# Gathering the tokens of eight experts at a time, with another order of steps around it

## The chip, the cores and the metric

One NeuronCore of a Trainium2 chip runs the kernel as one program. The metric is the device time of one launch in microseconds (us). A profiled execution of the kernel before gives, for each engine, what it did when: TensorE (PE, with its weight loads as PEld), VectorE (DVE), ScalarE (ACT), GpSimd (POOL) and SyncE (SP), which issues the transfers of weights.

## The reference

A trunk of two layers over 256 tokens of width 1024, all in f32. Each layer has a token mixer and a channel mixer, and both are modulated by six vectors that a product of a conditioning vector with `ada_w` gives:

```python
mod = silu(c) @ ada_w[l] + ada_b[l]              # sh1, sc1, g1, sh2, sc2, g2
h = rmsnorm(x, norm_mix_g[l]) * (1 + sc1) + sh1
proj = h @ w_in[l]                               # split among three kinds of attention heads
mix = concat([differential, sliding_window, dilated]) @ w_out[l]
x = x + g1 * mix
h = rmsnorm(x, norm_ffn_g[l]) * (1 + sc2) + sh2
x = x + g2 * moe(h)                              # after both layers: rmsnorm(x, final_norm_g)
```

`moe` has 4 groups of 4 experts. A router takes the best group of a token and in it the best two experts; each expert is `(silu(h @ w_gate) * (h @ w_up)) @ w_down` with w_gate and w_up 1024 x 512 and w_down 512 x 1024. Each of the 16 experts has some tokens, so all weights are read once: 283.63 MB of transfers in all.

## The kernel before

**Weights.** `Body.units` (L345) writes down, in the order of use, every piece of weights ("unit", mostly 512 KB). `Ring` (L137) issues them in that order on SP's queue. A unit goes to one of 29 ring tiles ("big"); the next transfer starts when the oldest unit is finished and its slot is free. Since SP issues in order, a unit that waits for its place holds up all behind it. Some units of the expert part don't take ring slots: HALVES (L32) names units, counted from the layer's first gate unit, that go to two tiles of the pool "w" (17 tiles of 128x512), and LENT (L33) units that go to a work tile of the pool "k" (11 tiles of 128x1024). Ring slots, "w" and "k" tiles serve everything else too.

**Order.** TensorE's instructions run in the order in which the code writes them. ScalarE's, VectorE's, GpSimd's and SP's are put in order by a planner with a cost model; `issue_after(i)` forces what is in its block behind instruction i of the same engine. For the mixer the written order is a list of names: START (before layer 1's mixer: S = split a unit of w_in into a high and a low fp32r part on ScalarE and VectorE, L761; X = transposes of x, L663; a = one step of an `ada_w` product for later modulation, four matmuls of 512 columns on two units, L450; R = the factor of the norm, L672), MIX (P = a unit of the input projection, twelve fp32r products; A, B, C = the three attentions) and TAIL (CT = transposes of q and k of the dilated heads, CF their scores and softmax, AM = transposes of the differential heads' output, B V/O and C V/O = probabilities times values, W = a unit of the output projection, d = a step of `ada_w` for the channel mixer, L524). The same list fixes the place of every unit in the stream (`pieces`, L416).

START of layer 1 is a generator (L729): it is advanced during the last expert of layer 0, whose last two quarters of columns (`combined`, L1451) are added to x between its steps.

**Router** (L1171). x is transposed and multiplied with the router's weights into one PSUM bank; four partial results are summed by a second product (`pl`) from an SBUF copy (L1195). `e` is a step of `ada_w` as `d` is. While the norm's factor r is made, ScalarE makes the high fp32r part of x * r (`xhi`, L1206); VectorE ranks the logits, counts each token's place in its expert (`pos`, at most 64 an expert), and makes the low part (`xlo`, L1246).

**Experts** (L1309). They run in 8 pairs j. `gather` turns tokens into slots by products with a one-hot matrix (VectorE's comparison of `pos` with 1..64, L1303): for each four experts, before pair j = 0, 2, 4, 6, 32 products of 256 columns, evicted with the modulation into two k tiles. Then come for each pair gate (`first`, L1361), the transposes and the down products of the pair before (L1407), `places` (transposes of the one-hots, L1338), up (L1361) and `combine`, which sends the results back to tokens by the transposed one-hots (L1428).

Of the kernel before, what the change touches and what calls it, by code (L numbers as in the profile page):

```python
# [9 lines left out]
F32 = mybir.dt.float32  # L10
F32R = mybir.dt.float32r
BF16 = mybir.dt.bfloat16
I32 = mybir.dt.int32
AF = mybir.ActivationFunctionType
OP = mybir.AluOpType
# [4 lines left out]
S = 256  # L20
KT = 8
NE = 16
CAP = 64
# [6 lines left out]
SCRATCH = 512  # L30
AHEAD = 2
HALVES = ((21, 27), (21, 27))  # L32
LENT = (((27, 32), (61, 62), (64, 65), (67, 68)),) * 2  # L33
NW = 17
A_START = 24

# [10 lines left out]
C_Z, C_CAUSAL, C_ID, C_CFAR, C_IOTA, C_LOW = (_AT[n].start for n in ("Z", "CAUSAL", "ID", "CFAR", "IOTA", "LOW"))  # L47
# [6 lines left out]

START = ["X c c R c c S00".split(), "S00 S01 X0 X1 S02 X2 X3 a a R".split()]
TAIL = """
CT0 CT1 d d d d CF0 AM1 CF1
W0 BV0 BV1 W1 BV2 BV3 BO0 BV4 W2 BV5 CV0 W3 BO1 CV1 CV2 W4 CO0 W5 W6  # L60
"""
MIX = [("""
P00 c P01 c P10 c c N P11 P02 P03 a a P12 L AT0 P13 a a AT1
# [2 lines left out]
P40 P41 BF1 a P42 AM0 P43 BF2 a a a H2 a  # L66
""" + TAIL).split(), ("""
P00 P01 P02 P03 P10 P11 AT0 P12 AT1 P13 AF0
P20 a AF1 P21 a AF2 P22 a P23 a
P30 AV0 P31 AV1 a AO0 BT0 P32 AV2 BT1 AO1 P33 AO2 BF0 a  # L70
P40 P41 BF1 P42 G2 AM0 P43 BF2 H2
""" + TAIL).split()]
# [127 lines left out]
class Body:  # L200
# [694 lines left out]
    def mixer(self, l):  # L895
        nc, ring, mod = self.nc, self.ring, self.mod
# [218 lines left out]

        acc = {}

        def wout(k, t):
            if k == 0 and t == 0:
                for tt in range(2):  # L1120
                    for hf in range(2):
                        acc[tt, hf] = self.acc.tile([128, 512], F32, name="acc")
            self.split_upto(l, 20 + k + AHEAD)
            mix, i = (T["mixa"], k) if k < 2 else (T["mixb"], k - 2) if k < 6 else (T["mixc"], k - 6)
            for hf in range(2):
                self.product(acc[t, hf], [m[:, i, blk(t)] for m in mix],
                             [p[:, 512 * hf:512 * hf + 512] for p in self.parts[20 + k]], k == 0, k == KT - 1)

        def w(k):
            if k < 6:  # L1130
                for t in range(2):
                    wout(k, t)
                return
            self.new_squares()
            for t in range(2):
                for k in (6, 7):
                    wout(k, t)
                for hf in range(2):
                    c = slice(512 * hf, 512 * hf + 512)
                    d = self.w()  # L1140
                    nc.vector.tensor_tensor(out=d, in0=acc[t, hf], in1=mod[l, 2][:, c], op=OP.mult)
                    nc.vector.tensor_tensor(out=self.x[t][:, c], in0=self.x[t][:, c], in1=d, op=OP.add)
                    self.square(t, hf, 512 * hf, 512 * hf + 512)
# [4 lines left out]
        for what in MIX[l]:  # L1148
            name, n = what.rstrip("0123456789"), what.lstrip("ABCFGHLMNOPSTVWacd")
# [21 lines left out]
    def router(self, l, dense):  # L1171
        nc, small = self.nc, self.one
        xt = {}
        for t in range(2):
            for i in range(2):
                xt[t, i] = self.w().rearrange("p (j c) -> p j c", j=4)
                p = self.transposes([self.x[t][:, 512 * i + 128 * j:512 * i + 128 * j + 128] for j in range(4)],
                                    _Named(self.acc, "acc"))
# [6 lines left out]
        ps = self.ps.tile([128, 512], F32, name="s")  # L1185
        for t in range(2):
            for i in range(2):
                for j in range(4):
                    nc.tensor.matmul(ps[32 * j:32 * j + 32, 128 * t:128 * t + 128], lhsT=self.wrs[:, 4 * i + j],
                                     rhs=xt[t, i][:, j], start=(i == 0), stop=(i == 1))  # L1190
        self.common(l, "e")
        pl = [ps[:, 256 + 20 * t:276 + 20 * t] for t in range(2)]
        for t in range(2):
            lt = self.w()[:, 0:128]
            nc.scalar.copy(lt, ps[:, 128 * t:128 * t + 128])  # L1195
            nc.tensor.matmul(pl[t], lhsT=lt, rhs=self.cb[:, C_SEL:C_SEL + 20], start=True, stop=True)
        self.common(l, "e")
        r = self.rstds(self.squares())
        if not dense:

            self.xhi, self.xlo = [[self.wk.tile([128, KT, 128], F32R, name="k") for t in range(2)] for _ in range(2)]
            xk = [self.x[t].rearrange("p (k c) -> p k c", k=KT) for t in range(2)]
            for i in range(2):
                for t in range(2):
                    c = slice(4 * i, 4 * i + 4)
                    nc.scalar.activation(self.xhi[t][:, c], xk[t][:, c], AF.Copy, scale=r[t])  # L1206
        lg = small.tile([128, 2, 20], F32, name="lg")
        for t in range(2):
            nc.vector.scalar_tensor_tensor(out=lg[:, t], in0=pl[t], scalar=r[t],
                                           in1=self.rbias, op0=OP.mult, op1=OP.add)  # L1210
# [7 lines left out]
                                in1=lf.unsqueeze(3).to_broadcast([128, 10, 4, 4]), op=OP.is_ge)  # L1218
# [8 lines left out]
        if not dense:  # L1227
            ab = small.tile([128, 2, 4, 4], BF16, name="ab")
            nc.vector.scalar_tensor_tensor(out=ab, in0=rank[:, :, 1:5], scalar=1.5, op0=OP.is_lt, op1=OP.mult,
                                           in1=og.unsqueeze(3).to_broadcast([128, 2, 4, 4]))  # L1230
# [8 lines left out]
                                           in1=ab, op0=OP.add, op1=OP.mult)  # L1239
# [57 lines left out]

    def one_hot(self, b):

        one = self.w(F32R).rearrange("p (t e s) -> p t e s", t=2, e=4)  # L1300
        iota = self.cb[:, C_IOTA:C_IOTA + CAP].unsqueeze(1).to_broadcast([128, 4, CAP])
        for t in range(2):
            i = self.nc.vector.tensor_tensor(out=one[:, t], in0=iota, op=OP.is_equal,  # L1303
                                             in1=self.pos[:, t, 4 * b:4 * b + 4].unsqueeze(2).to_broadcast([128, 4, CAP]))
        self.hot[b] = one.rearrange("p t e s -> p t (e s)")
        return i


    def moe(self, l):  # L1309
        nc, ring = self.nc, self.ring  # L1310
# [1 line left out]
        sh, sc, g = self.mod[l, 3], self.mod[l, 4], None  # L1312
        xt, G, U, pts, gates, act = {}, {}, {}, {}, {}, {}

        def gather(b, k2):

            if k2 == 0:
                if b:
                    self.one_hot(b)
                xt[b] = [self.wk.tile([128, 4, S], F32, name="k") for _ in range(2)]  # L1320
            one = hot[b]
            p = self.pt.tile([128, 512], F32, name="t").rearrange("p (k s) -> p k s", k=2)
            for kk in range(2):
                n = 0
                for t in range(2):
                    for part in (self.xhi, self.xlo):
                        nc.tensor.matmul(p[:, kk], lhsT=part[t][:, 2 * k2 + kk], rhs=one[:, t],  # L1327
                                         start=(n == 0), stop=(n == 3))
                        n += 1
            for kk in range(2):  # L1330
                self.modulate(xt[b][k2 // 2][:, 2 * (k2 % 2) + kk], p[:, kk], sc, sh, 2 * k2 + kk, 1 - k2 % 2)

        def places(j):

            p = self.pt.tile([128, 512], F32, name="t")
            hf = hot[j // 2][:, :, 128 * (j % 2):128 * (j % 2) + 128]
            for t in range(2):
                nc.tensor.transpose(p[:, 128 * t:128 * t + 128], hf[:, t].bitcast(F32), self.ident)  # L1338
            for t in range(2):
                nc.tensor.matmul(p[:, 256:288], lhsT=hf[:, t],  # L1340
                                 rhs=self.ghl[:, t].rearrange("p u e -> p (u e)"), start=(t == 0), stop=(t == 1))
            pt = self.w(F32R)[:, 0:S]
            nc.scalar.copy(pt, p[:, 0:256])
            gs = self.small.tile([128, 1], F32, name="gs")
            for u in range(2):
                e = 2 * j + u
                r = slice(64 * u, 64 * u + 64)
                nc.vector.tensor_reduce(out=gs[r], in_=p[r, 256 + e:288:16], axis=AX.X, op=OP.add)
            pts[j], gates[j] = pt, gs

        def first(kind, store, j, hh):

            if hh == 0:
                store[j] = self.ps.tile([128, 512], F32, name="s")
            x = xt[j // 2]
            w = [ring.take2((kind, l, 2 * j + u, hh)) for u in range(2)]
            for kk in range(2):
                k = 2 * hh + kk
                for u in range(2):
                    c = (j % 2) * 128 + 64 * u  # L1360
                    nc.tensor.matmul(store[j][64 * u:64 * u + 64, :], lhsT=x[k // 4][:, k % 4, c:c + 64],  # L1361
                                     rhs=w[u][kk], start=(k == 0), stop=(k == KT - 1))
            ring.done(2)

        def gates_of(j, between=None):

            if j % 2:
                first("gate", G, j, 0)
                first("gate", G, j, 1)
                if between:  # L1370
                    between()
            else:
                gather(j // 2, 0)
                gather(j // 2, 1)
                first("gate", G, j, 0)
                gather(j // 2, 2)
                if between:
                    between()
                first("gate", G, j, 1)
                gather(j // 2, 3)  # L1380
            first("gate", G, j, 2)
            first("gate", G, j, 3)
            silu(j)
# [267 lines left out]
```

## Time and profile before

| | us |
|---|---|
| median of 3 runs | 758.12 (757.98 to 759.51) |
| profiled execution | 756.71 |
| its span, first to last instruction | 754.8 |
| TensorE busy | 712.9 |
| VectorE busy | 342.6 |
| ScalarE busy | 211.7 |
| GpSimd busy | 65.7 |
| TensorE's weight loads busy (beside the products) | 372.4 |

A busy time counts an engine's instructions and not what they waited for. Matmul records overlap, so TensorE's busy time is no measure of how near it is to its peak. Of the transfers, the weight queue (q1) carried 282.33 MB; the mean rate over the span was 376 GB/s. TensorE's clock has two levels in this profile, granted 1.00 (2.4 GHz) and 0.50 (1.2 GHz).

### The profile page before, as it was taken

How to read it: one execution, taken by the hardware profiler on the slowest of the kernel's cores; microseconds unless marked ns; L12 is line 12 of the kernel's file. 1: busy time of each engine (PE TensorE's matmuls, PEld its weight loads, DVE VectorE, ACT ScalarE, POOL GpSimd, SP SyncE). 2: the span in 40 equal slices, each digit the busy share in tenths (PEclk: the TensorE clock that was granted, in tenths of full speed). 3: DMA queues.
4: the chain of work that ended last, by engine and by line, in shares of the span. 5: the costliest groups of instructions: out<-in, count | busy, mean ns of one | idle time of the engine just before them, and what ended most of it. 6: DMA issues, size and time to landing. Idle time of an engine off the chain costs nothing.

```text
span 754.8 us, 10672 instructions
## 1 busy us (share of the span) xinstructions
PE 712.9 (94%) x3790; PEld 372.4 (49%) x3790; DVE 342.6 (45%) x940; ACT 211.7 (28%) x482; POOL 65.7 (9%) x89
## 2 busy tenths in 40 slices
PE   6899898999999999999989999897999999999993
PEld 2565675754353353353346668675435335344341
DVE  4587697354042333133357869637213313332234
ACT  2345345432021111111134645643211111112011
POOL 1010234001000000000001121500100000000002
PEclk9899999998999999999989999998999999999997
DMA  9999999998989999999999996879799999999991
GB/s 354 409 409 407 407 409 409 408 379 330 382 336 409 409 410 409 409 409 410 400 406 408 406 404 211 339 241 393 278 363 373 409 409 409 409 410 409 409 382 63
DMA packets 82745, 283.63 MB, mean 376 GB/s; under 512 B 9198, under 2 KB 9327, under 8 KB 82684
## 3 DMA queue, kind: packets, MB, share of 16 engines
q1 hardware_dynamic: 82186, 282.33, 95.6%
q8 instruction: 32, 0.52, 0.3%
q10 hardware_dynamic: 434, 0.53, 0.2%
q14 instruction: 29, 0.24, 0.1%
q0 software_dynamic: 64, 0.02, 0.0%
HBM read 281.78 MB, written 1.06 MB: 375 GB/s over the span
## 4 chain that ended last, share of the span: by engine, by line
PE 84%; DVE 8%; ACT 3%; DMA 2%; issue 1%; SPq 0%; DVEq 0%; ACTq 0%
PE s L1361 30%; PE acc L1407 13%; PE acc L718 6%; PE acc L719 5%; PE acc L720 5%; PE t L1327 5%; PE acc L1428 4%; PE t L803 3%; PE acc L457 3%; DVE k L775 2%; PE acc L1442 2%; DMA big<-in_w_in_dram 1%; PE acc L1459 1%; DMA big<-in_ada_w_first_dram 1%; PE s L884 1%
## 5 line engine op out<-in xcount | busy, mean ns | idle before, releaser
L1361 PE MATMUL s<-big,k 128*64 128x512 f32 x976 | 228.2, 598 | 0.0
L1361 PEld LDWEIGHTS s<-big,k 128*64 128x64 f32 x976 | 67.4, 136 | 118.6 <-issue 104.8
L1413 DVE SCALAR_TENSOR_TENSOR w<-acc,gs,g 128x512 f32<-128x512 f32 x28 | 21.0, 751 | 155.3 <-PE acc L1407 153.8
L1407 PE MATMUL acc<-big,w 128*64 128x512 f32 x384 | 84.4, 592 | 0.0
L718 PE MATMUL acc<-k 128*128 128x512 f32 (+1 forms) x176 | 69.8, 397 | 3.8 <-ACT k L707 3.6
L775 DVE TENSOR_TENSOR k<-big,k 128x1024 fp32r<-128x1024 f32 (+1 forms) x56 | 66.0, 1186 | 15.7 <-ACT k L770 11.4
L720 PE MATMUL acc<-k 128*128 128x512 f32 (+1 forms) x176 | 66.8, 380 | 0.0
L719 PE MATMUL acc<-k 128*128 128x512 f32 (+1 forms) x176 | 66.3, 377 | 0.0
L770 ACT CAST k<-big 128x1024 fp32r<-128x1024 f32 (+1 forms) x56 | 53.9, 985 | 35.0 <-PE acc L719 26.8
L1407 PEld LDWEIGHTS acc<-big,w 128*64 128x64 f32 x384 | 27.6, 137 | 54.8 <-issue 52.8
L1392 DVE TENSOR_TENSOR w<-w,s 128x512 f32<-128x512 f32 x16 | 11.0, 688 | 84.3 <-PE s L1361 84.3
L718 PEld LDWEIGHTS acc<-k 128*128 128x128 f32 x176 | 33.6, 191 | 19.8 <-issue 7.3
L1327 PEld LDWEIGHTS t<-w,k 128*128 128x128 f32 x256 | 35.4, 205 | 16.0 <-issue 8.1
L1417 ACT CAST w<-w 128x512 fp32r<-128x512 f32 x28 | 17.3, 619 | 89.6 <-DVE w L1413 89.6
L835 ACT ACTIVATE w<-w,nm 128x128 f32<-128x128 f32 (+1 forms) x80 | 35.4, 445 | 22.4 <-DVE nm L833 20.2
L1327 PE MATMUL t<-w,k 128*128 128x256 f32 x256 | 39.8, 306 | 1.8 <-DVE w L1303 1.5
L724 ACT ACTIVATE k<-t,mod,mod 128x256 f32<-128x256 f32 x32 | 16.3, 561 | 85.4 <-PE t L1327 85.4
L1398 ACT COPY w<-t 128x512 f32<-128x512 f32 x16 | 9.4, 586 | 107.9 <-PE t L803 107.9
L720 PEld LDWEIGHTS acc<-k 128*128 128x128 f32 x176 | 33.7, 191 | 8.0 <-DVE k L891 1.6
L719 PEld LDWEIGHTS acc<-k 128*128 128x128 f32 x176 | 33.8, 192 | 4.9
L803 PE MATMUL t<-cb,w 128*128 128x128 f32 x224 | 33.6, 278 | 2.0 <-ACT w L860 0.7
L1430 DVE TENSOR_TENSOR x<-x,acc 128x512 f32<-128x512 f32 x56 | 34.9, 682 | 0.2
(269 smaller groups left out, 857.1 us busy)
## 6 DMA issues: line engine op xcount, KB each, us to landing
big<-in_expert_w_up_dram SPq DMA_DIRECT2D x126, 512.0 KB, 10.2
big<-in_expert_w_gate_dram SPq DMA_DIRECT2D x118, 512.0 KB, 10.2
big<-in_expert_w_down_dram SPq DMA_DIRECT2D x108, 512.0 KB, 10.2
big<-in_ada_w_dram SPq DMA_DIRECT2D x80, 512.0 KB, 10.2
big<-in_w_in_dram SPq DMA_DIRECT2D x32, 512.0 KB, 10.2
big<-in_ada_w_first_dram SPq DMA_DIRECT2D x16, 512.0 KB, 10.2
big<-in_w_out_dram SPq DMA_DIRECT2D x16, 512.0 KB, 9.0
w<-in_expert_w_down_dram SPq DMA_DIRECT2D x20, 256.0 KB, 7.4
```

Source lines behind the costliest of these rows:

```text
L718: self.nc.tensor.matmul(p, lhsT=xh, rhs=wh, start=start, stop=False)
L719: self.nc.tensor.matmul(p, lhsT=xh, rhs=wl, start=False, stop=False)
L720: self.nc.tensor.matmul(p, lhsT=xl, rhs=wh, start=False, stop=stop)
L770: nc.scalar.copy(hi, w)
L775: nc.vector.tensor_tensor(out=lo, in0=w, in1=hi.bitcast(F32), op=OP.subtract)
L803: self.nc.tensor.transpose(p[:, i], b, self.ident)
L835: nc.scalar.activation(e[:, h], e[:, h], AF.Exp, bias=nm[:, g:g + 1], scale=scale, accum_out=sm[:, g:g + 1])
L1327: nc.tensor.matmul(p[:, kk], lhsT=part[t][:, 2 * k2 + kk], rhs=one[:, t], start=(n == 0), stop=(n == 3))
L1361: nc.tensor.matmul(store[j][64 * u:64 * u + 64, :], lhsT=x[k // 4][:, k % 4, c:c + 64], rhs=w[u][kk], start=(k == 0), stop=(k == KT - 1))
L1407: nc.tensor.matmul(ps[hf][64 * u:64 * u + 64, :], lhsT=act[j][:, f, 64 * u:64 * u + 64], rhs=w[u][hf], start=(f == 0), stop=(f == 3))
L1428: nc.tensor.matmul(p, lhsT=pts[j][:, 128 * t:128 * t + 128], rhs=part, start=(n == 0), stop=(n == 1))
L1430: nc.vector.tensor_tensor(out=self.x[t][:, c], in0=self.x[t][:, c], in1=p, op=OP.add)
```

## The change

- LENT: the first lent stretch has three units instead of five; the two others go to ring tiles.
- START of layer 1 runs five steps `a` instead of two, and the third projection (P20 to P23) one instead of four.
- TAIL: the four steps `d` are put singly and in a pair between CT0, CT1, CF0, AM1 and W0, and CF1 comes behind W0.
- `w(6)`: the last two units of the output projection are multiplied for one half of the columns, then for the other.
- Router: both last steps `e` come behind the products `pl`, and ScalarE's `xhi` behind the copies.
- One-hots are made for eight experts at a time in two "w" tiles, and the gather runs before j = 0 and j = 4 only, with 32 products of 512 columns each and evictions of 512 columns into four k tiles. `places` makes its own one-hots of 128 columns.

```diff
-LENT = (((27, 32), (61, 62), (64, 65), (67, 68)),) * 2
+LENT = (((27, 30), (61, 62), (64, 65), (67, 68)),) * 2
-START = ["X c c R c c S00".split(), "S00 S01 X0 X1 S02 X2 X3 a a R".split()]
+START = ["X c c R c c S00".split(), "S00 S01 X0 X1 a S02 X2 a X3 a a R a".split()]
-CT0 CT1 d d d d CF0 AM1 CF1
-W0 BV0 BV1 W1 BV2 BV3 BO0 BV4 W2 BV5 CV0 W3 BO1 CV1 CV2 W4 CO0 W5 W6
+CT0 d CT1 d CF0 AM1 d d W0 CF1
+BV0 BV1 W1 BV2 BV3 BO0 BV4 W2 BV5 CV0 W3 BO1 CV1 CV2 W4 CO0 W5 W6
-P20 a AF1 P21 a AF2 P22 a P23 a
+P20 AF1 P21 a AF2 P22 P23
...
-                for k in (6, 7):
-                    wout(k, t)
                 for hf in range(2):
+                    for k in (6, 7):
+                        wout(k, t, (hf,))
...
-        self.common(l, "e")
         pl = [ps[:, 256 + 20 * t:276 + 20 * t] for t in range(2)]
         for t in range(2):
             lt = self.w()[:, 0:128]
-            nc.scalar.copy(lt, ps[:, 128 * t:128 * t + 128])
+            copied = nc.scalar.copy(lt, ps[:, 128 * t:128 * t + 128])
             nc.tensor.matmul(pl[t], lhsT=lt, rhs=self.cb[:, C_SEL:C_SEL + 20], start=True, stop=True)
+        self.common(l, "e")
         self.common(l, "e")
...
+            with self.tc.issue_after(copied.ins):
+                for i in range(2):
+                    for t in range(2):
+                        c = slice(4 * i, 4 * i + 4)
+                        nc.scalar.activation(self.xhi[t][:, c], xk[t][:, c], AF.Copy, scale=r[t])
...
+        self.hot[b] = [self.w(F32R) for t in range(2)]
         for t in range(2):
+            i = self.hot_of(self.hot[b][t], t, 8 * b, 8)
         return i
+
+    def hot_of(self, out, t, e0, n):
+        iota = self.cb[:, C_IOTA:C_IOTA + CAP].unsqueeze(1).to_broadcast([128, n, CAP])
+        return self.nc.vector.tensor_tensor(out=out.rearrange("p (e s) -> p e s", e=n), in0=iota, op=OP.is_equal,
+                                            in1=self.pos[:, t, e0:e0 + n].unsqueeze(2).to_broadcast([128, n, CAP]))
...
+            if k % 2 == 0:
+                xt[b].append(self.wk.tile([128, 2, 512], F32, name="k"))
+            p = self.pt.tile([128, 512], F32, name="t")
+            n = 0
+            for part in (self.xhi, self.xlo):
                 for t in range(2):
+                    nc.tensor.matmul(p, lhsT=part[t][:, k], rhs=hot[b][t], start=(n == 0), stop=(n == 3))
+                    n += 1
+            self.modulate(xt[b][k // 2][:, k % 2], p, sc, sh, k, 1 - k % 2)
...
-            hf = hot[j // 2][:, :, 128 * (j % 2):128 * (j % 2) + 128]
+            hf = self.w(F32R)[:, 0:S].rearrange("p (t c) -> p t c", t=2)
+            for t in range(2):
+                self.hot_of(hf[:, t], t, 2 * j, 2)
...
+            ks = range(KT) if j % 4 == 0 else ()
+            for k in ks[0:4]:
+                gather(j // 4, k)
+            first("gate", G, j, 0)
+            for k in ks[4:6]:
+                gather(j // 4, k)
+            if between and ks:
+                between()
+            first("gate", G, j, 1)
+            if between and not ks:
+                between()
+            for k in ks[6:8]:
+                gather(j // 4, k)
             first("gate", G, j, 2)
             first("gate", G, j, 3)
```

## Rows read from the trace of the kernel before

**Rows 1.** Page, the span in 40 equal slices: GB/s moved in each.
```profile
GB/s 354 409 409 407 407 409 409 408 379 330 382 336 409 409 410 409 409 409 410 400 406 408 406 404 211 339 241 393 278 363 373 409 409 409 409 410 409 409 382 63
```

**Rows 2.** Timeline of SP's queue, several stretches: start us, us, issue, tile<-tensor, count.
```profile
205.68 0.33 SPq L154 DMA_DIRECT2D k<-in_expert_w_up_dram  x1
211.46 0.80 SPq L154 DMA_DIRECT2D big<-in_expert_w_up_dram  x2
...
361.96 0.33 SPq L154 DMA_DIRECT2D big<-in_expert_w_up_dram  x1
380.31 2.37 SPq L154 DMA_DIRECT2D big<-in_ada_w_dram  x4
...
716.46 0.33 SPq L154 DMA_DIRECT2D big<-in_expert_w_up_dram  x1
```

**Rows 3.** DMA issues, all (first) and that of 211.46 (second): KB each, us to landing.
```profile
big<-in_expert_w_up_dram SPq DMA_DIRECT2D x126, 512.0 KB, 10.2
...
big<-in_expert_w_up_dram SPq DMA_DIRECT2D x1, 512.0 KB, 3.8
```

**Rows 4.** Chain that ended last, in order of time: start us, us, what, instructions.
```profile
271.19 1.91 PE t L1327 x16
...
274.97 1.15 PE t L1327 x8
...
367.27 7.02 PE s L1361 x32
...
441.16 0.99 PE acc L457 x8
...
443.05 0.23 PE acc L718
...
721.86 7.02 PE s L1361 x32
```

**Rows 5.** Timeline of TensorE and VectorE, tail of layer 0; idle before in brackets.
```profile
116.09 3.64 PE L532 MATMUL acc<-big,cb 128*32 128x512 f32 x32
118.28 0.71 DVE L1068 COPY w<-t 128x256 f32<-128x256 f32 x2
122.23 1.46 PE L1074 MATMUL s<-w 64*128 64x256 f32 x8 [1.48 <-DVE mx L829]
...
127.82 0.40 PE L720 MATMUL acc<-k,w 128*128 128x512 f32 x1
```

**Rows 6.** Timeline, first down of layer 0, then router and first gather of layer 1.
```profile
205.04 4.03 PE L1407 MATMUL acc<-k,w 128*64 128x512 f32 x17
...
518.37 1.06 PE L1189 MATMUL s<-w,wrs 128*32 128x128 f32 x32
520.49 0.24 ACT L1195 COPY w<-s 128x128 f32<-128x128 f32 x1
522.61 0.39 DVE L1209 SCALAR_TENSOR_TENSOR lg<-s,newton,rbias 128x20 f32<-128x20 f32 x2 [2.14 <-PE s L1196]
525.56 0.76 DVE L1303 TENSOR_TENSOR w<-cb,pos 128x256 fp32r<-128x256 f32 x2
526.23 3.25 DVE L1246 SCALAR_TENSOR_TENSOR k<-x,newton,k 128x256 fp32r<-128x256 f32 x8
536.26 3.65 PE L1361 MATMUL s<-big,k 128*64 128x512 f32 x16
```

**Rows 7.** Windows: us, busy (count) of PE, PEld, DVE, ACT, POOL, PEclk, DMA share, GB/s.
```profile
413.00:432.00 19.00, 19.00 (x92) 13.62 (x90) 16.32 (x49) 10.59 (x25) 4.87 (x4) 1.00 1.03 406
523.40:530.10 6.70, 4.41 (x23) 3.79 (x19) 6.21 (x21) 1.12 (x3) 0.20 (x1) 0.50 0.94 372
566.00:570.00 4.00, 4.00 (x22) 1.29 (x19) 0.08 (x1) 0.00 (x0) 0.00 (x0) 1.00 0.71 258
```

**Rows 8.** Timeline of TensorE, start of layer 1.
```profile
394.40 3.20 PE L457 MATMUL acc<-big,cb 128*32 128x512 f32 x16
399.77 0.50 PE L718 MATMUL acc<-k 128*128 128x512 f32 x1 [1.52 <-ACT k L707]
```

More of the change, by code (lines that the diff above doesn't have):

```diff
@@ L1116, in mixer, with wout @@
         acc = {}
-        def wout(k, t):
+        def wout(k, t, hfs=(0, 1)):
             if k == 0 and t == 0:
@@ L1124, in wout @@
             mix, i = (T["mixa"], k) if k < 2 else (T["mixb"], k - 2) if k < 6 else (T["mixc"], k - 6)
-            for hf in range(2):
+            for hf in hfs:
                 self.product(acc[t, hf], [m[:, i, blk(t)] for m in mix],
@@ L1202, in router @@
             xk = [self.x[t].rearrange("p (k c) -> p k c", k=KT) for t in range(2)]
[L1203 to L1206, printed above, removed]
+            with self.tc.issue_after(copied.ins):
[3 more added lines that the diff above has]
+                        nc.scalar.activation(self.xhi[t][:, c], xk[t][:, c], AF.Copy, scale=r[t])
         lg = small.tile([128, 2, 20], F32, name="lg")
@@ L1298, in one_hot @@
     def one_hot(self, b):
-        one = self.w(F32R).rearrange("p (t e s) -> p t e s", t=2, e=4)
-        iota = self.cb[:, C_IOTA:C_IOTA + CAP].unsqueeze(1).to_broadcast([128, 4, CAP])
+        self.hot[b] = [self.w(F32R) for t in range(2)]
         for t in range(2):
-            i = self.nc.vector.tensor_tensor(out=one[:, t], in0=iota, op=OP.is_equal,
-                                             in1=self.pos[:, t, 4 * b:4 * b + 4].unsqueeze(2).to_broadcast([128, 4, CAP]))
-        self.hot[b] = one.rearrange("p t e s -> p t (e s)")
-        return i
+            i = self.hot_of(self.hot[b][t], t, 8 * b, 8)
+        return i
+    def hot_of(self, out, t, e0, n):
+        iota = self.cb[:, C_IOTA:C_IOTA + CAP].unsqueeze(1).to_broadcast([128, n, CAP])
+        return self.nc.vector.tensor_tensor(out=out.rearrange("p (e s) -> p e s", e=n), in0=iota, op=OP.is_equal,
+                                            in1=self.pos[:, t, e0:e0 + n].unsqueeze(2).to_broadcast([128, n, CAP]))
     def moe(self, l):
@@ L1313, in moe, with gather @@
         xt, G, U, pts, gates, act = {}, {}, {}, {}, {}, {}
-        def gather(b, k2):
-            if k2 == 0:
+        def gather(b, k):
+            if k == 0:
                 if b:
                     self.one_hot(b)
[L1320 to L1324, printed above, removed]
-                for t in range(2):
[L1326 to L1331, printed above, removed]
+                xt[b] = []
+            if k % 2 == 0:
[3 more added lines that the diff above has]
+            for part in (self.xhi, self.xlo):
+                for t in range(2):
+                    nc.tensor.matmul(p, lhsT=part[t][:, k], rhs=hot[b][t], start=(n == 0), stop=(n == 3))
+                    n += 1
+            self.modulate(xt[b][k // 2][:, k % 2], p, sc, sh, k, 1 - k % 2)
         def places(j):
             p = self.pt.tile([128, 512], F32, name="t")
-            hf = hot[j // 2][:, :, 128 * (j % 2):128 * (j % 2) + 128]
+            hf = self.w(F32R)[:, 0:S].rearrange("p (t c) -> p t c", t=2)
+            for t in range(2):
+                self.hot_of(hf[:, t], t, 2 * j, 2)
             for t in range(2):
@@ L1354, in first @@
                 store[j] = self.ps.tile([128, 512], F32, name="s")
-            x = xt[j // 2]
+            x = xt[j // 4]
             w = [ring.take2((kind, l, 2 * j + u, hh)) for u in range(2)]
@@ L1359, in first @@
                 for u in range(2):
-                    c = (j % 2) * 128 + 64 * u
-                    nc.tensor.matmul(store[j][64 * u:64 * u + 64, :], lhsT=x[k // 4][:, k % 4, c:c + 64],
+                    c = (j % 4) * 128 + 64 * u
+                    nc.tensor.matmul(store[j][64 * u:64 * u + 64, :], lhsT=x[k // 2][:, k % 2, c:c + 64],
                                      rhs=w[u][kk], start=(k == 0), stop=(k == KT - 1))
@@ L1365, in gates_of @@
         def gates_of(j, between=None):
[L1367 to L1380, printed above, removed]
+            ks = range(KT) if j % 4 == 0 else ()
[11 more added lines that the diff above has]
+                gather(j // 4, k)
             first("gate", G, j, 2)
```

## The prediction

> **What bounds the kernel now.** I read the rate of transfers over 40 slices first, then the issues of the weight queue, then the chain of waits. The weights come at 409 GB/s in most slices; only behind each layer's mixer does the rate fall (to between 330 and 382 in the first layer, 211 and 393 in the second) [rows 1]. There the 29 ring slots are full, and a transfer starts when a matmul frees a slot.
>
> Inside the experts the chain is matmuls without a hole, and still they only just follow the stream. The last "up" unit of layer 0 is issued at 361.96 [rows 2] and lands 10.2 later [rows 3], at 372.2; the run of 32 matmuls that eats it begins at 367.27 and takes 7.02 [rows 4], so its last quarter starts at 372.5. Layer 1 repeats it: issue 716.46, landing 726.7, use 721.86 + 5.27 = 727.1 [rows 2 to 4]. The slack is 0.4 us in both. So matmul time saved inside an expert part gives at most 0.4 us, and the end moves only as far as the stream moves. The stream moves only where it stands still for a slot: when the first experts begin earlier. That is the view for every edit: what it does to the first experts' time, and from there to the stream.
>
> **The change part by part.** Times are shifts against the profiled execution, minus is earlier. Call d what the first gather, from one-hot to the last gate product, loses.
>
> *Tail (both layers).* In layer 0 four ada_w steps run from 116.09 to 119.7, then CF0, AM1, a wait, CF1 at 122.23 (waited 1.48), and W0 ends at 128.05, part of it at half clock [rows 5]. After it: CT0, one step (0.9), CT1, one step, about 118.0; CF0 needs the key copy that VectorE ends near 118.7 [rows 5], so TensorE waits 0.7; then CF0 and AM1 1.1 (as from 119.7 to the wait before 122.23), two steps 1.8, W0 from 121.7. Its 12 products at 0.23 (the spacing in the chain [rows 4]) are 2.7, and CF1, 1.4, comes behind: 125.8 against 128.05. I take -1.8 (bounds -2.5 and +1.5, the last if VectorE's queue brings AM1's low half late, for which W0's second half waits). CF1's softmax starts 2.5 later, but its probabilities are transposed only behind two W steps (5.5 us) and all of BV, so that is covered; without this cover the 2.5 would show. In layer 1 there is no half clock to win; the wait before CF1 and a new wait before CF0 are near equal: -0.5 (-1.5 to +1.5).
>
> *Last products of the output projection by halves.* Half 0 of the last token block ends three products of 0.23 earlier; VectorE's multiply and add of it start by as much earlier, and half 1 follows: -0.6 in each layer (0 to -0.7).
>
> *Router.* The 32 logit matmuls end at 519.43; the first copy runs at 520.49, behind a step of ada_w on TensorE and two scalings on ScalarE, and VectorE gets both logits at 522.61 [rows 6]. After the change: copy 0.25, product 0.4, copy 0.25, product 0.4, four handovers of 0.1: 519.43 + 1.7 = 521.1, against 522.6. The two steps that were between now run beside VectorE's ranking, and so do the scalings. -1.4 (-1.8 to 0).
>
> *First gather, d.* Before: one-hots at 525.56, last gate product at 536.26 + 3.65 = 539.9 [rows 6]: 14.3 us. After: two one-hots over 512 elements, 0.65 each where two over 256 took 0.76 in all; then the low half of the first two columns, two of the eight steps that take 3.25 [rows 6], 0.8 with the handover 0.9; then 32 products of 512 columns at 0.23 are 7.3; the gate products, four runs of 1.75 (a quarter of 7.02 [rows 4]), 7.0. Eviction is now one tile of 512 for each k, on ScalarE and VectorE in turn; VectorE still has six low-half steps in front of it, 2.4, of which some 0.5 shows. Sum 1.3 + 0.9 + 7.3 + 7.0 + 0.5 = 17.0: d = +2.8 (bounds +1.8, VectorE in the best order, and +6.2, below).
> The Trainium skill prices such a product lower: TensorE: Matmul & The Clock Gate, section Back-to-back issue gap, gives about 131 ns for a product of 512 columns in a sustained stream with its weight loads. By it 32 products would be an estimated 4.2 us, d about -0.3, and by the formula below the time would be some 6 us lower than I forecast. The chain shows 0.23 for the same shape and kind [rows 4], and the row decides.
>
> *Later gathers.* Four experts took 1.91 + 2 x 1.15 = 4.2 us [rows 4]; the next eight now take 7.3 at once and the other two none. TensorE gains 4.2 in the third pair's step and loses 3.1 in the fifth. This lies behind the stream's last stall or is eaten by it: 0 by itself. The small one-hots for the places, two VectorE instructions a pair, lie in an engine that is mostly idle there: 0, with TensorE waiting for them at most 0.4 a pair, less than the stream gives back.
>
> *Two lent tiles fewer.* Two "down" units that sat in work tiles now hold ring slots until the first down's last quarter. SP issues in order, so the unit before the lent "up" unit, and it behind, wait for that: before, this lent unit went at 205.68, the next at 211.46 [rows 2]; a transfer into an empty queue lands after 3.8 [rows 3]. The first down ends at 205.04 + 4.03 = 209.1 [rows 6]; +3.6, +3 x 1.28 (a unit's 512 KB at 409 GB/s) makes the unit of 211.46 land at 216.5, against 215.3: +1.2 for an unmoved first down. Stalls still to come there swallow about 1.7 of it (bounds 0.5 and 2.1): -0.5. In layer 1 the same sum is +2.9, and the stalls that go (258 of 409 GB/s over 4 us [rows 7] are 1.5 alone) are 1.8 to 3.8: I take 0 (-0.9 to +1.1).
>
> *Start of layer 1.* Five steps of ada_w instead of two: three more times four matmuls and three pairs of transfers, moved ahead of w_in's. The two steps there now take 3.20 at half clock [rows 8]; one at full clock is 0.99 [rows 4]. The first two of the five stand ahead of the products of which VectorE adds the sum to x: TensorE waits for their data, and those products and the transposes of x wait behind it, some 1 us each. The data of the last bind: before, the first ada_w unit is issued at 380.31 [rows 2] as the fourth of the layer and lands about 388; the fifth step's second unit is the thirteenth, nine places of 1.28 on, 399.6 with queue gaps up to 400.0. That step ends at 400.9, and the first projection goes at 401 instead of 399.77 [rows 8]: +1.2 beside the stream's shift. The pushed w_in unit, six transfers or 7.7 us later, is needed three units of 12 products, 8.2 us, behind that start: covered. In return three steps of 0.99 leave the third projection. There TensorE is busy 19.0 of 19 us, VectorE 16.3 [rows 7]: -2.5 of the 3.0 (bounds -3.0, and 0 if VectorE's queue holds that stretch).
>
> **Sum.** First down of layer 0: -1.8 - 0.6 - 1.4 + d = d - 3.8. Stream at the end of layer 0: d - 4.3. First projection of layer 1: d - 3.1. First down of layer 1: + (-2.5 - 0.5 - 0.6 - 1.4) + d = 2d - 8.1. Stream at the end: the same, and the slack of 0.4: 2d - 8.5. With d = 2.8: -2.9. The end behind the stream (last products, norm, output) is not touched. Profiled execution 756.7 (span 754.8): 753.8. The median of the runs stands 1.4 above that execution: **755.2**.
>
> **Rivals.**
> 1. *More of it comes through* (d = 1.8, all 3.0 of the steps, tail of layer 1 -1.5, each router -1.8): 3.6 - 8.5 - 0.5 - 1.0 - 0.8 = -7.2: 750.9. For it: the rate is far under 409 behind both mixers. Against: each term at its best.
> 2. *The moved steps are not paid back*: VectorE, not TensorE, holds the third projection (16.3 of 19 us busy in the rows, its queue in order), so the 2.5 is gone: -0.4: 757.7. No change.
> 3. *Slower: the first gather at half clock.* Place: the gather and gate products behind the router. Before, the clock is at 0.50 from 523.4 to 530.1 (1.2 GHz) with TensorE busy 4.4 of 6.7 us [rows 7], and there much of it was idle or waiting. The 512-wide gather is all matmul; if the same 6.8 us lie on it, half of them are lost, d = 2.8 + 3.4 = 6.2, twice: 12.4 - 8.5 = +3.9: 762.0. It decides from d = 4.25 (no change) and is measurable from d = 5. For it: the router still leaves TensorE idle for the ranking, now in one stretch, as the steps run before it. Against: TensorE is busier just before, and the old gather paid part of it too. The Trainium skill, TensorE: Matmul & The Clock Gate, section Why this matters for your kernels, warns of idle gaps between bursts of matmuls in just this way; the row of 523.4 agrees that the clock fell there.
> 4. *The order written is not the order run*: ScalarE's, VectorE's and SP's orders are a planner's; if it puts the copies or lent transfers elsewhere, the terms cancel: 758.
>
> **How the numbers follow.** Forecast 0.42 (own range 753 to 756.6), rival 1 0.20, rival 2 0.18, rival 3 0.13, rival 4 0.07. A measurement of this kernel tells 0.2%, 1.5 us, from no change. Faster by more: most of the forecast (0.38), rival 1, a little of 2 and 4 (0.04): 0.62. Slower: rival 3 and some of 2 and 4: 0.17. The rest, 0.21, no change. The range 749.5 to 762 leaves out the best of rival 1 and the worst of rival 3, under 2 in 10.
>
> **What would show it.** Logits on VectorE 1.4 us after the logit matmuls end instead of 3.2; the first gather and gates at 17 us; gathers of 7.3 us in every fourth pair; slots' waits moved to the first down's end, and the "up" unit behind the lent one landing near 216; the first projection of layer 1 right behind an ada_w step; TensorE waiting for "up" units in the last pair. Wrong it is if the last "up" still has slack, if the third projection does not shorten by 2 to 3 us, or if the clock's low stretch covers the first gather.

## The result and the profile after

Slower: 802.52 us median of 4 runs (801.64 to 803.94), against 758.82 (757.98 to 759.73) for the kernel before; the ratio is 1.0577 [1.0555, 1.06]. The profiled execution took 803.94, its span 802.2. The forecast was 755.2 and its range ended at 762: the sign was wrong, and the time lies 47 us above the forecast, 40 above the range.

First the page of after: the granted clock and the rate of transfers in 40 slices, 20 us each.
```profile
PEclk9899999999999999999899999999989999999998
GB/s 354 409 410 406 409 409 408 391 329 333 298 403 408 410 409 409 409 410 402 405 408 406 236 184 239 260 329 238 338 313 411 409 408 355 408 410 408 403 104 57
```
The weights still come at 409 in the experts, as in [rows 1], so the stream is not what broke. The next view is what TensorE waited for (total us, times, longest), the longest such wait of after:
```profile
PE t L1341 <- DVE w L1308: 36.2, 14, 2.6
```
L1341 is the transpose of a pair's places, L1308 the small one-hot that the change makes for it. Fourteen of the 16 pairs (all but the first of each layer) wait 2.6 us each, 36.2 in all. This is the timeline of one of them in after, the end of the first down of layer 0 (start, us, engine, line; in brackets the idle time before and who ended it):
```profile
207.31 1.89 PE L1409 MATMUL acc<-big,w 128*64 128x512 f32 x8
208.41 1.61 DVE L1415 SCALAR_TENSOR_TENSOR w<-acc,gs,g 128x512 f32<-128x512 f32 x2 [12.93 <-PE acc L1409]
209.94 1.46 DVE L1422 TENSOR_TENSOR w<-w 128x512 fp32r<-128x512 f32 x2
211.31 0.49 DVE L1308 TENSOR_TENSOR w<-cb,pos 128x128 fp32r<-128x128 f32 x2
211.74 0.65 PE L1341 MATMUL t<-cb,w 128*128 128x128 f32 x2 [2.55 <-DVE w L1308]
212.56 8.37 PE L1364 MATMUL s<-big,k 128*64 128x512 f32 x32
```
and the same place before:
```profile
208.29 1.58 DVE L1413 SCALAR_TENSOR_TENSOR w<-acc,gs,g 128x512 f32<-128x512 f32 x2 [12.93 <-PE acc L1407]
209.00 0.44 PE L1338 MATMUL t<-cb,w 128*128 128x128 f32 x2
209.79 1.46 DVE L1420 TENSOR_TENSOR w<-w 128x512 fp32r<-128x512 f32 x2
```
VectorE stood idle for 12.93 us and had nothing to do; but places() is called behind down(), the planner kept that order, and in VectorE's queue the one-hots stand behind the two weighted evictions (L1415), which need down's last products, and the two low halves (L1422), which need ScalarE's casts in between. Before, the transposes took a slice of a one-hot made long ago and followed down at once. The second loss is in the last row: these 32 products took 8.37 and not 7.09. The windows of after (us, busy of PE, PEld, DVE, ACT and POOL, granted clock, DMA share, GB/s) show why:
```profile
209.00:212.00 3.00, 0.45 (x4) 0.29 (x3) 2.60 (x6) 1.24 (x2) 0.00 (x0) 0.96 0.59 199
212.00:216.00 4.00, 4.00 (x14) 1.58 (x15) 0.31 (x2) 0.37 (x1) 0.00 (x0) 0.60 0.67 258
212.00:382.00 170.00, 157.00 (x698) 60.24 (x699) 40.80 (x78) 18.63 (x32) 0.00 (x0) 0.97 1.01 399
569.00:720.00 151.00, 138.06 (x598) 52.17 (x596) 34.97 (x67) 17.07 (x29) 1.48 (x2) 0.94 0.98 385
```
and of before:
```profile
212.00:382.00 170.00, 170.00 (x834) 71.43 (x830) 48.60 (x90) 22.55 (x43) 0.95 (x1) 1.00 1.02 404
569.00:720.00 151.00, 151.00 (x740) 63.08 (x738) 41.62 (x78) 20.45 (x39) 1.48 (x2) 1.00 1.03 408
```
Behind the hole the clock is granted at 0.60 for 4 us, that is mostly at 1.2 GHz. Over the two expert stretches the mean is 0.97 and 0.94, and 1.00 before, so 0.03 x 170 + 0.06 x 151 = 14 us of matmul time are lost to the clock. It did not fall behind every hole: in this execution behind eight of the fourteen (the 32 "up" products then mostly take 8.37 to 9.80), while behind six it stayed at 1.00 (mostly 7.09).

By stage, from the first down's end to the end of the last "up": 209.19 to 396.97 in layer 0, 187.8 us against 165.2 before; in layer 1 588.60 to 776.39, again 187.8 against 165.2. That is 45 of the 47 us between the spans. The first down of layer 0 ends at 209.19 against 209.07, and from the last "up" of layer 0 to the first down of layer 1 it is 191.6 against 189.4.

### The profile page after: what moved, and what is told of

Same layout as the page of the kernel before. It is cut to its first block, busy times and chain, and to the rows that moved or that the text cites. A ratio compares the mean times of both kernels' runs of the same rounds, so it can differ in the third digit from the quotient of the medians.

```text
span 802.2 us, 10404 instructions
## 1 busy us (share of the span) xinstructions
PE 724.8 (90%) x3662; PEld 363.1 (45%) x3662; DVE 345.8 (43%) x948; ACT 209.8 (26%) x466; POOL 65.4 (8%) x89
## 3 DMA queue, kind: packets, MB, share of 16 engines
HBM read 281.78 MB, written 1.06 MB: 353 GB/s over the span
## 5 line engine op out<-in xcount | busy, mean ns | idle before, releaser
L1364 PE MATMUL s<-big,k 128*64 128x512 f32 x976 | 241.7, 629 | 0.0
L1364 PEld LDWEIGHTS s<-big,k 128*64 128x64 f32 x976 | 71.0, 144 | 134.7 <-issue 129.7
L1415 DVE SCALAR_TENSOR_TENSOR w<-acc,gs,g 128x512 f32<-128x512 f32 x28 | 21.0, 750 | 172.0 <-PE acc L1409 170.5
L1409 PE MATMUL acc<-big,w 128*64 128x512 f32 x400 | 88.2, 592 | 0.0
L1330 PE MATMUL t<-w,k 128*128 128x512 f32 x128 | 36.6, 423 | 4.9 <-DVE w L1308 2.2
L1419 ACT CAST w<-w 128x512 fp32r<-128x512 f32 x28 | 17.3, 618 | 90.3 <-DVE w L1415 90.3
L1341 PE MATMUL t<-cb,w 128*128 128x128 f32 x32 | 8.0, 334 | 36.2 <-DVE w L1308 36.2
L803 PE MATMUL t<-cb,w 128*128 128x128 f32 x224 | 34.0, 280 | 1.1 <-ACT w L860 1.1
L803 PEld LDWEIGHTS t<-cb,w 128*128 128x128 f32 x224 | 24.7, 141 | 19.0 <-issue 14.4
```

The lines of the kernel that those rows point to most:

```text
L803: self.nc.tensor.transpose(p[:, i], b, self.ident)
L1330: nc.tensor.matmul(p, lhsT=part[t][:, k], rhs=hot[b][t], start=(n == 0), stop=(n == 3))
L1409: nc.tensor.matmul(ps[hf][64 * u:64 * u + 64, :], lhsT=act[j][:, f, 64 * u:64 * u + 64], rhs=w[u][hf], start=(f == 0), stop=(f == 3))
L1415: nc.vector.scalar_tensor_tensor(out=ds[-1], in0=p, scalar=gates[j], in1=g[:, 512 * hf:512 * hf + 512], op0=OP.mult, op1=OP.mult)
```

## Experiments

Theory Q: the one-hots' place in VectorE's queue costs 36 us, and the clock behind these holes some 14 more. Rival S: two lent tiles fewer starve the stream. Rival C: the clock falls for another reason. Each run was timed beside the kernel before (medians 757.2, 758.3 and 759.0 in the three groups); ratios are to it.

**The one-hots earlier (e1).** In after, the two `hot_of` calls of places() go to a function small_hot(), which is called ahead of down():
```diff
...
+            hf = small_hot(j)
             if j:
                 parts = down(j - 1)
-            places(j)
+            places(j, hf)
```


> After, with one thing moved: the two small one-hots of a pair stand ahead of the pair before's down on VectorE's queue instead of behind its evictions. Theory Q (the places wait in VectorE's queue: 14 waits of 2.6 us, 36.2 us in all, and some 14 us of matmuls at half clock that follow those holes): both go, 802.5 - 36 - 11 to 14 = 752 to 757. Rival S (two lent tiles fewer starve the weight stream, the waits of the places are only where TensorE happens to stand): 790 or more. Rival C (the waits go, but the clock falls for another reason, the 512-wide gather or the fewer lent tiles): 766, with the up runs of 32 still at 8.3 to 9.8 us in places.


Measured 764.82, ratio 1.0087 [1.0058, 1.0115]. One moved line is worth 37 us. The same place:
```profile
207.85 1.89 PE L1412 MATMUL acc<-big,w 128*64 128x512 f32 x8
208.96 1.61 DVE L1418 SCALAR_TENSOR_TENSOR w<-acc,gs,g 128x512 f32<-128x512 f32 x2 [12.40 <-PE acc L1412]
209.67 0.44 PE L1344 MATMUL t<-cb,w 128*128 128x128 f32 x2
```
No wait, and the clock is at 1.00 from 212 to 382. S falls; C's 766 would fit the time as well, but the clock at 1.00 speaks against it. Q holds, but 8 to 13 us more are left than it said. Most of them lie at the end of each layer, where TensorE now waits for weights: the last "down" and "up" take 9.5 and 9.8 us in layer 0, 10.7 and 9.8 in layer 1, against 7.0 and 7.1 before. Two rows of it, in layer 0:
```profile
361.45 2.35 PE L1412 MATMUL acc<-big,w 128*64 128x512 f32 x8 [0.21 <-DMA big<-in_expert_w_down_dram]
371.69 2.35 PE L1367 MATMUL s<-big,k 128*64 128x512 f32 x8 [0.20 <-DMA big<-in_expert_w_up_dram]
```

**The late one-hots alone (e2).** In before, places() makes its own:
```diff
-            hf = hot[j // 2][:, :, 128 * (j % 2):128 * (j % 2) + 128]
+            hf = self.w(F32R)[:, 0:S].rearrange("p (t c) -> p t c", t=2)
+            for t in range(2):
+                self.hot_of(hf[:, t], t, 2 * j, 2)
```


> Before, with one thing of the change alone: each pair makes its own small one-hots in places, behind down's evictions, where before they were slices of the four-expert one-hot; gathers, lent tiles, orders as before. Theory Q: 758.8 + 14 x 2.6 + 8 to 14 for half clock = 803 to 809. Rival S (lent tiles): 759, within 2. Rival C: 795, the waits without the clock's part.


Measured 799.77, ratio 1.0579 [1.0526, 1.0631]: this part alone loses as much as the whole change. Its wait is the same:
```profile
PE t L1345 <- DVE w L1311: 36.3, 14, 2.6
```
The clock took less in this execution than in after's (1.00 from 212 to 382 and 0.98 from 569 to 720; it fell behind two of the same fourteen holes), and the time came out between C (795) and Q (803 to 809). Its four runs spread from 796.5 to 805.9.

**Before with own one-hots, early (h2).** The edits of e1 and e2 together, on before.


> Before, with each pair's own small one-hots as in the change, but ahead of the pair before's down on VectorE's queue (the late ones cost 758 to 800). Theory Q: only the place in the queue costs, so 758, within 1.5. Rival (the two more VectorE instructions a pair or the tile that they hold cost by themselves): 762 or more.


Measured 757.80, ratio 0.999 [0.997, 1.001]. The instructions cost nothing; only their place in the queue does.

**The one-hots half way (e4).** In after's down(), between the two weighted evictions and the low halves:
```diff
...
+            hf = small_hot(j + 1)
             for d in ds:
                 his.append(self.w(F32R))
...
```


> After, with the small one-hots of a pair between down's two weighted evictions and its two low halves on VectorE's queue. Theory Q: the one-hots end 0.5 us behind the second weighted eviction, some 1.3 us after down's last matmul, so a wait of 1.3 instead of 2.6 a pair: 36 becomes 18, and 802.5 - 18 = 784 with the clock's part whole, 770 with none of it left. Rival S: 800 or more. If only the presence of the one-hots counts and not their place in the queue: 802.


The wait is as Q has it, here of the same pair:
```profile
209.23 0.44 PE L1344 MATMUL t<-cb,w 128*128 128x128 f32 x2 [1.17 <-DVE w L1308]
```
In the list of waits, and in the window of layer 0's experts, it reads
```profile
PE t L1344 <- DVE w L1308: 16.2, 14, 1.2
```
```profile
212.00:382.00 170.00, 162.97 (x748) 63.17 (x746) 46.15 (x89) 20.45 (x35) 0.95 (x1) 1.00 1.03 406
```
but the time is 767.01, ratio 1.0121 [1.0088, 1.0153], lower than the 770 that was the least expected. Holes of 1.2 us leave the clock at 1.00, and most of the 16 us lie where e1 waits for weights instead: from the first down to the last "up" of layer 0 it is 169.9 us, against 166.4 in e1. The cost of such a wait is not linear. An estimate for layer 0: e1's 166.4 less the 5.2 that its last "down" and "up" wait for weights are 161.2 us without any wait; seven holes of 1.17 make 169.4 (measured 169.9), seven of 2.6 make 179.4 (179.9 in h1, below, at full clock). So the stream covers the first 5 us in a layer, the rest shows in full, and the longer holes bring the clock with them (187.8 in after).

**The wait filled (h1).** After as it is; TensorE works on data it has, for nobody, while it waits:
```diff
+            if j:
+                idle = self.ps.tile([128, 512], F32, name="s")
+                for _ in range(18):
+                    nc.tensor.matmul(idle[:, 0:S], lhsT=pts[j - 1][:, 0:128], rhs=pts[j - 1], start=True, stop=True)
             for t in range(2):
                 nc.tensor.transpose(...)
```


> After as it is, one-hots late, but TensorE works through 18 products of 256 columns (0.13 each, 2.3 us) that nothing reads between a pair's last down product and its places; VectorE's order is unchanged, so the places come no earlier. Theory Q in two parts: the 36 us of waits stay (now filled), and the 14 us of half clock that follow the holes go: 802.5 - 14 = 788, granted clock at 1.00 in the experts. Rival (the clock falls for another reason than the holes): 802, or more where the idle products push the places.


Measured 787.95, ratio 1.0386 [1.0346, 1.0427]: 14.6 us less than after. VectorE's queue is unchanged (its one-hots at 210.83 here), the places come no earlier, and the run of 32 is back at 7.09:
```profile
208.63 2.42 PE L1343 MATMUL s<-w 128*128 128x256 f32 x18
211.17 0.53 PE L1345 MATMUL t<-cb,w 128*128 128x128 f32 x2
211.76 7.09 PE L1368 MATMUL s<-big,k 128*64 128x512 f32 x32
```
and the windows of both expert stretches have the clock at 1.00:
```profile
212.00:382.00 170.00, 168.88 (x816) 72.67 (x814) 44.05 (x85) 20.15 (x35) 0.00 (x0) 1.00 1.02 404
569.00:720.00 151.00, 150.09 (x724) 64.48 (x724) 37.41 (x71) 18.30 (x31) 1.48 (x2) 1.00 1.01 400
```
That is the clock's share, 14.6 us; the wait's is the rest of the 37.

**The orders with the old gather (e3).** START, third projection, tail, output-projection halves and router of the change; gather, one-hots and lent tiles of before.


> The change without its gather: new tail, output-projection halves, router and start of layer 1; gathers of four experts, slices for the places and the lent tiles as before. Theory Q with the prediction's other terms (end = -8.5 + 2d with d = 0): 750.3, within 747 to 753. Rival M (the moved steps at the start of layer 1 cost as much as they give): 753 to 757. Rival N (the tail's and router's time lies behind the stream anyway): 758, within 1.5.


Measured 747.98, ratio 0.9862 [0.9832, 0.9892]: faster than both kernels. The formula of the prediction, with d = 0, said 750.3 (758.8 - 8.5).

**Lent tiles (g1).** e3 with one number changed:
```diff
-LENT = (((27, 32), (61, 62), (64, 65), (67, 68)),) * 2
+LENT = (((27, 30), (61, 62), (64, 65), (67, 68)),) * 2
```


> The orders alone (748.0 before this run) and, beside them, the change's two lent tiles fewer; gathers of four experts still. Theory L (the prediction's sum for the lent tiles was too low: the late units cost 1.2 in layer 0 and 2.9 in layer 1 and the stalls do not swallow them): 751 to 752. Rival (the stalls swallow them, as predicted at -0.5 and 0; what is late in the corrected change comes with the gather itself): 748, within 1.


Measured 754.69, ratio 0.9941 [0.9912, 0.9971], against 0.9862: 6.0 us slower, with some 3 of uncertainty, and more than Theory L said. The traces show less of it: from the first down to the last "up" 165.9 against 165.2 in both layers, its last run of 32 at 7.82 for weights. But g1's profiled execution is the quickest of its five (750.46 to 755.88) and e3's the slowest of its four (746.50 to 751.54), so these two traces do not show what the times lose.

**Idle products ahead of the first gather (g2 on e3, g3 on e1).** Three products of 512 columns ahead of the router's counting products and five behind it.


> The orders alone, with eight products of 512 columns that nothing reads, three ahead of the router's counting products and five behind, where TensorE otherwise waits for VectorE's ranking. Theory K (the first gather runs at half clock because TensorE idled ahead of it: the 16 products of the first gather take 4.2 and 3.6 us in the orders' profile where those of the later gathers take 2.07): 748.0 - 1.5 to 2.1 in each layer = 744 to 745. Rival (the clock falls for another reason, or the filler delays the gather by as much): 748 to 749.

> The change with early one-hots (764.8), with the same eight idle products ahead of the first gather. Theory K: the first 12 products of the 512-column gather take 5.1 and 5.2 us there, 0.43 each against 0.23 at full clock, so 2.3 to 2.4 us a layer come back: 760. Rival (512-column products are slow by themselves, or the evictions hold them): 764 to 765, the first 12 products still at 5.1.


g2: 749.21, ratio 0.986 [0.983, 0.9889], the same as e3, where Theory K said 744 to 745. g3: 761.97, ratio 1.0045 [1.0019, 1.0072] against 1.0087, 3.2 us with some 3 of uncertainty, where K said 4.8. The clock does stay up. The first gather of layer 0 in e1, and a window inside it:
```profile
167.38 5.12 PE L1330 MATMUL t<-w,k 128*128 128x512 f32 x12 [1.10 <-DVE w L1308]
173.37 1.19 PE L1330 MATMUL t<-w,k 128*128 128x512 f32 x4 [0.87 <-ACT k L724]
```
```profile
168.00:170.00 2.00, 2.00 (x5) 1.46 (x6) 2.00 (x6) 0.48 (x1) 0.00 (x0) 0.63 1.02 408
```
and the same in g3:
```profile
167.66 3.86 PE L1335 MATMUL t<-w,k 128*128 128x512 f32 x12
172.38 1.19 PE L1335 MATMUL t<-w,k 128*128 128x512 f32 x4 [0.87 <-ACT k L724]
```
```profile
168.00:170.00 2.00, 1.90 (x8) 1.23 (x7) 2.00 (x6) 0.51 (x1) 0.00 (x0) 1.00 1.03 414
```
But the fourth chunk still waits 0.87 for an eviction, and 12 products at full clock still take 3.86 and not 12 x 0.23 + 0.17 = 2.9: the weight loads among them wait for the second one-hot (0.41), VectorE's low halves (0.21 twice) and an eviction (0.37). From the first product to the last gate product it is 18.5 and 18.0 us in e1 and 17.3 and 17.3 in g3, so the half clock costs 1.3 and 0.7. The gather of four loses more to it: 13.8 and 13.9 in e3, 12.1 and 12.1 in g2. So the half clock is real but explains nothing of d, the difference of the two gathers: with the clock at 1.00 in both, 17.3 against 12.1, it is larger (5.2) than without the idle products (4.8 and 4.0).

**The single orders, each put back in e3 (g4, h3, h4).** g4 has the old START and third projection, h3 the old tail, h4 the old router.


> The orders with the old start of layer 1 and the old third projection (tail, output-projection halves and router as in the change). The prediction priced the new start at +1.2 and the shorter third projection at -2.5, so without both 748.0 + 1.3 = 749.3. Rival 2 of the prediction (the steps moved are not paid back): 746.8 to 748. If the new start is worth more, all 3.0 of the steps: 751.

> The orders with the old tail (start of layer 1, output-projection halves and router new). The prediction priced the new tail at -1.8 in layer 0 and -0.5 in layer 1, so 748.0 + 2.3 = 750.3. The orders' trace shows W0 ending 3.4 earlier in layer 0, which would make it 751.5 to 753. If the tail's time is covered anyway: 748.

> The orders with the old router (one ada_w step between the logits and their copies, the scalings of x ahead of the second copy; tail and start of layer 1 new). The prediction priced the new router at -1.4 a layer: 748.0 + 2.8 = 750.8. If the first gather then runs at the higher clock, as the steps stand closer to it, some of it comes back: 749.


g4: 750.94, ratio 0.9903 [0.9877, 0.993], so the new start is worth 3.1. h3: 751.46, ratio 0.9908 [0.9875, 0.9941], the tail 3.5. h4: 756.29, ratio 0.9957 [0.994, 0.9975], the router 7.2, where at most 2.8 was expected. Each difference has some 3 us of uncertainty; their sum, 13.8, is more than the 10.5 that they give together, so they are not simply additive.

## Why the prediction was wrong

**The step that failed** is "The small one-hots for the places ... lie in an engine that is mostly idle there: 0, with TensorE waiting for them at most 0.4 a pair". Measured: 2.6 a pair and the clock behind it, 37 us in all (after against e1). The number of the engine's busy share was right and had no bearing: VectorE runs its queue in order, and an instruction that needs nothing of down stands behind two that need down's last products and two that need ScalarE. All of it was to be read in the trace of before: the rows shown above have VectorE's evictions from 208.29, its low halves from 209.79 to 211.25, and TensorE's transposes at 209.00. The prediction asked what the instructions take, and not where they stand. No rival had it either.

The 802.5 is then made up, by ratios: orders -10.5 (e3); lent tiles +6.0 (g1 against e3); the gather of eight with early one-hots +11.1 (e1 against g1); the late one-hots +37 (after against e1). Each step starts where the last one ends, so the sum is the measured +43.7 by construction and confirms nothing; each of the first three has some 3 us of uncertainty.

Point by point:
- *Tail, -1.8 and -0.5.* Right in kind; 3.5 by the time. In layer 0 W0 ends at 124.4 and not 128.06 [rows 5], and the next output products start 3.4 earlier: the old wait of 1.48 is now 0.40, and W0 runs at full clock, 2.9 us for the 12 products where it took 4.4 (granted 1.00 from 122 to 124, against 0.50 from 124.0 to 127.4 before).
```profile
118.65 0.71 PE L1074 MATMUL s<-w 64*128 64x128 f32 x8 [0.40 <-DVE w L1068]
...
121.52 0.50 PE L718 MATMUL acc<-k,w 128*128 128x512 f32 x1
...
124.14 0.39 PE L720 MATMUL acc<-k,w 128*128 128x512 f32 x1
```
  In layer 1 the new wait before CF0 is 1.80, and the prediction had no term for the clock behind it: in e3, e1, g2, g3 and after the two steps `d` that follow take 3.0 to 3.6 us, in e4, g1, g4, h1 and h4 1.92. From CT0 to the next output products it is 15.2 in the first five and 13.5 in the others, against 13.7 with the old tail: +1.5 or -0.2 where -0.5 was said. The rows of e3, then of g4:
```profile
471.44 3.56 PE L532 MATMUL acc<-big,cb 128*32 128x512 f32 x16
...
472.51 1.92 PE L532 MATMUL acc<-big,cb 128*32 128x512 f32 x16
```
- *Output projection by halves, -0.6.* Not to be seen. From the last product's start to the last transposes of x it is 3.1 us in layer 0 before (159.49 to 162.60) and after (156.12 to 159.24): VectorE's multiply of half 0 still starts 0.20 behind the last product, as before.
- *Router, -1.4.* The term itself is right (the counting products 4.9 earlier, 3.4 of that from the tail: 1.5), but by the time the router is worth 7.2 for both layers together. In h4 TensorE idles longer ahead of the gather, the clock is at 0.50 from 170 to 174 and from 520 to 530, through gate products too, and from the first gather to the last gates it takes 15.0 and 15.1 us against 13.9 and 14.0 in e3. That difference of some 1.1 a layer was not in the sum; 2 x (1.5 + 1.1) is 5.2 of the 7.2, which have 3 of uncertainty. Against before it is no gain: there, with the old router, the same stretch takes 13.6 and 13.9.
- *First gather, d = +2.8.* From the counting products to the step behind the gates it is 19.9 and 19.3 us in e1, 14.9 and 15.0 in e3: d = 5.0 and 4.3, inside the bounds (1.8 to 6.2). (At the first down's end e1 stands 5.4 and 5.6 further back; the rest of these is 0.4 ahead of the router of layer 0 and 1.4 ahead of the first projection of layer 1.) That is near rival 3's 6.2, but not by its half clock. In layer 1 of after the clock was at 1.00, and it took 18.0 us from first product to last gate, the same as in e1, where it was at 0.58:
```profile
546.82 3.86 PE L1330 MATMUL t<-w,k 128*128 128x512 f32 x12 [1.10 <-DVE w L1308]
547.19 3.25 DVE L1247 SCALAR_TENSOR_TENSOR k<-x,newton,k 128x256 fp32r<-128x256 f32 x8
551.38 0.80 DVE L726 TENSOR_SCALAR k<-t,mod,mod 128x512 f32<-128x512 f32 x1
552.23 1.20 PE L1330 MATMUL t<-w,k 128*128 128x512 f32 x4 [1.55 <-DVE k L726]
555.23 2.10 PE L1330 MATMUL t<-w,k 128*128 128x512 f32 x8
```
  The products took 3.9 + 1.1 + 2.0 + 2.1 = 9.1 where 7.3 was said, the eviction behind VectorE's queue 1.55 where 0.5 was said, the gates 7.3 where 7.0 was; only the first product came sooner, 0.84 behind the start of the one-hots where 2.2 was said. (The prediction's own 17.0 less 14.3 is 2.7, not 2.8.) It is the same mistake in small: the eviction stands behind eight low halves and the first reductions of the gates.
- *Later gathers, 0.* Nearly right: the prediction left out the seventh pair's saving, but the stream takes it. In e1 TensorE saves the four-expert gathers of the third and the seventh pair and does one long one in the fifth, and what it saves it stands waiting for weights at the end of the layer. From the first down to the last "up" e1 takes 166.4 and 167.9, against 165.2 before, 0.7 of it by the lent tiles in g1's trace.
- *Two lent tiles fewer, -0.5 and 0.* By the times wrong by some 6 us in all, with 3 of uncertainty. Against the end of the first down, the "up" unit behind the lent one lands 6.2 us later in e3 (and before) and 8.0 in g1, and the last "up" of the layer still lands 1.6 later in g1 (164.0 against 162.4): the stalls do not swallow it. Of these 1.6 e3's slack, 1.1 where before had 0.4, takes 1.0, and 0.7 shows. Why the timed runs lose 6 where these traces show 0.7 a layer stays open.
- *Start of layer 1, +1.2 and -2.5.* Net -1.3 said, -3.1 measured, with 3 of uncertainty; rival 2, that it is not paid back, would be +1.2. The shorter third projection is there: from its first product to the fourth projection's it takes 15.8 us in e3, 18.1 before, -2.3 where -2.5 was said. The +1.2 is not settled: from the last "up" to the first projection it is 25.6 in e3, 25.5 before and 23.2 in g4.
- *End = 2d - 8.5.* With d = 0 it gave 750.3 for e3, which measured 748.0. With 2d = 9.3 and 6 for the lent tiles it gives +6.8 for e1, against +6.6 by the ratio; with 3 us of uncertainty on the parts, and the misses above, that so small a difference remains is luck.

## What to carry to other kernels

An engine's busy share says nothing of when a new instruction on it runs: look for the instruction ahead of it in the queue, and for what that one waits. Work that depends on nothing belongs ahead of the first instruction that has to wait, in the written order; one line moved was worth 37 us here, 5%. And a hole in TensorE can cost more than its length: 2.6 us holes had a second price of 1 us each on average at the lower clock in after (14.6 us over 14 holes), which idle products in the hole won back. And that price varies from one execution to the next: in e2's profile the same holes lost some 3 us to the clock.

## What the runs showed of the hardware

Holes of 2.6 us in otherwise full matmul work, 27 to 30 us apart (35 where a gather lies between), were followed by stretches at half clock behind eight of 14 holes in after's profile and behind two in e2's; holes of 1.2 us at the same places were followed by none. Products that nobody reads, run in the hole, took 14.6 us off the program although the places came no earlier; ahead of the first gather they held the clock at 1.00 too and shortened gather and gates by 1.7 and 1.8 us in e3's kernel, but its time did not change within 3 us; why is not shown.
